# A decoder trunk on one core: norm factor as exp(-ln/2), priorities for short work, and two more pairs of projections

## The chip, the core and the metric

The kernel runs on one core of a Trainium2 chip. Its engines are TensorE (matmuls, with a sequencer that also loads the stationary operand), VectorE, ScalarE, GpSimd and SyncE; in the profile they are PE (and PEld for weight loads), DVE, ACT, POOL and SP. The metric is the device time of one execution in microseconds (us); lower is better. Before the change it is 1003.29 us, the median of three runs (1003.1 to 1003.29).

## What is computed

One layer of a decoder over 528 tokens (16 learned ones ahead of 512), 1024 channels, all in float32:

```python
u = rmsnorm(h, mix_norm_w)
proj = u @ w_in                                  # pool, z, x|B|C, dt, gates
y_pool = pool_mixer(u_pool, ...) @ w_pool_up
xbc = silu(causal_depthwise_conv(xbc, conv_w, conv_b))     # 4 taps
...                                              # 8 groups, each: 256 channels of x, 128 of B, 128 of C
y = (y_diag + y_off) + xs * d_skip               # the chunked scan
y = y * silu(z)
yg = yg * rsqrt(mean(yg * yg, per group) + EPS)  # the norm factor of this text
y_ssd = (yg * norm_w) @ w_ssd_out
h = h + (gate_pool * y_pool + gate_ssd * y_ssd) @ w_o
h = h + relu(rmsnorm(h, mlp_norm_w) @ w_ff1) ** 2 @ w_ff2
out = rmsnorm(h, final_norm_w)[16:]
```

## The kernel before

**Precision.** A float32 operand is split into a high part (ScalarE's cast, `whi`) and the rest (VectorE's subtraction, `wlo`), and a product is three matmuls: high by high, high by low, low by high. `block()` (L115) loads one 128x1024 weight block over SyncE's queue and splits it (L111, L113), with priority 100. A projection of 128 output channels (`proj`, L208) is one such block: 8 steps along the contraction, 48 matmuls of 264 columns for the 528 tokens, or 24 of 512.

**The order of the work.** The program is written in the order below, and the Tile framework then orders each engine's instructions itself: where several are ready it takes the one that was written first, and `tc.high_priority(n)` counts an instruction as written n places earlier. `tc.issue_after(i)` (and `after`, L101, for several) puts an instruction behind another one.

**The scan.** `group_tiles` (L447) gives each of the eight groups its tiles: x (`xc`, two buffers), B (`bt`), C (`ct`) and `zt`. `weave` (L729) goes by turns through the steps of `ssd(g)` (L591) and of `group_proj(g + 1)` (L530), so the projections of the next group fill TensorE while the scan of this one waits for the other engines; in group 4 the first half of the output product (`out_half`), in group 7 the rest of it (`out_part`, L839) stands beside them. `ssd` turns B and x by TensorE, makes `eb` and the decays (Exp on ScalarE, L633, L644, L645; before them Relu, L638, and VectorE's L641), the products of C and B (L656), the states (L663 to L673: ScalarE's copy `st0`, then VectorE's chain of three steps), the masked decays (L676), y (L685 to L698), the sum of squares (L703 to L710), the norm factor `rs` (L712: ScalarE's Sqrt; L714: VectorE's reciprocal in four pieces) and the normed y with its two parts `yh`, `yl` (L718 to L722).

**Pairs.** For x of groups 4 to 7 (`X_PAIRS`, L50) the two projections are done together by `pair` (L494): Strassen's seven products of half-size blocks in place of eight (`MULTIPLY`, L468), 12 matmuls of 264 columns each. Its weights are four quarters and four sums of quarters (`t1`, `s3`, `t2`, `t4`) that `weight_sums_at` (L790) has made earlier by DMAs on GpSimd's queue, some of them adding in memory; `pair_operands` (L472) loads them on SyncE's queue, two products to a block. Each product is taken out of PSUM by ScalarE or VectorE (L510 to L525) into two raw tiles, `ra` and `rb` of the pool `stg` (`raw_pair`, L527), because a bank is used again by the product after the next. `conv` (L434) then reads the raw tiles. A plain projection's `conv` reads PSUM itself. `BC_PAIRS` (L51) names the groups whose B and C would be such a pair; it is empty.

**Sums of weights.** `sets` (L761) lists what is to be summed: two sets of the pairs of the scan (`fx`), then thirteen of the MLP; `SETS_AT` (L54) says how many are made beside which group (11 in all), and L1190 makes the rest after the scan. A set of `fx` or `f1` is eight DMAs of 512 KB, one of `f2` four.

**The end of the scan.** `out_part` sums the last y products: for the first two output blocks the products with y 12 and 13 come late and alternate between both sums (L876 to L881), then `add` (L866) copies each sum out of its PSUM buffer (ScalarE, L868) and adds it to memory by GpSimd's queue (L869). The PSUM pool of these sums has two buffers.

Of the kernel before, what the change touches and what calls it, by code (L numbers as in the profile page):

```python
# [16 lines left out]
SEQ = 512  # L17
# [4 lines left out]
G = 8  # L22
# [28 lines left out]
BC_PAIRS = ()  # L51
# [13 lines left out]
def kernel(ctx: ExitStack, tc, xT, x, w, fx, f1, f2, vec, fnw, out):  # L65
# [428 lines left out]
    def pair(kind, g, r):  # L494
# [3 lines left out]
        one, two = HF  # L498
        for m, f, n, start, stop in MULTIPLY:
# [10 lines left out]
            if m == "b11":  # L510
                act.copy(r[0][:, one], o)
            elif m == "b21":
                dve.tensor_tensor(r[0][:, one], r[0][:, one], o, op=ALU.add)
            elif m == "t2":
                second_product[g] = at
                act.activation(r[1][:, one], o, AF.Copy, scale=-1.0)
            elif m == "t1":
                act.copy(r[1][:, two], o)
                yield
            elif m == "s3":  # L520
                dve.tensor_tensor(r[1][:, two], r[1][:, two], o, op=ALU.subtract)
            elif m == "b22":
                dve.tensor_tensor(r[1][:, one], r[1][:, one], o, op=ALU.add)
            else:
                act.copy(r[0][:, two], o)  # L525
# [4 lines left out]
    def group_proj(g, cur, gate=None):  # L530
# [20 lines left out]
        both = g in BC_PAIRS  # L551
        for kind, ts, paired in (("b", bcs, both), ("x", xs, g in X_PAIRS)):
            if paired:
                r = raw_pair(kind, g)
                yield from pair(kind, g, r)
                for (dst, t, skip), src in zip(ts, r):
                    conv(dst, src[:, skip:], t)
                yield
            else:
                for t in ts:  # L560
                    plain(*t)
                    filled.setdefault(g - 1, mm[0])
                    yield
            if both:
                i = 0 if kind == "b" else 1
                ps = psum2(f"pz{g}_{i}")[:, :SEQ]
                z_half(ps, i)
                z_ready[g] = act.activation(zt[:, i, :], ps, AF.Silu)
                yield
        if both:  # L570
            return
# [19 lines left out]
    def ssd(g, cur):  # L591
# [38 lines left out]
        for j in range(2):  # L630
            js = slice(64 * j, 64 * j + 64)
            with after((z_ready if g in X_PAIRS else x_ready)[g], late_cast[0] if g == G - 1 else None):
                act.activation(eb[js, :, :], ap[js, :, j, :], AF.Exp)  # L633
# [33 lines left out]
        y_first[g] = st0 = act.copy(flat(st[0]), pv[0])  # L667
# [44 lines left out]
        act.activation(rs, pn, AF.Sqrt, bias=eps, scale=1.0 / 256)  # L712
        for c in range(4):
            dve.reciprocal(rs[:, ctok(c)], rs[:, ctok(c)])  # L714
# [11 lines left out]
    late_cast, last_state = [None], {}  # L726
# [112 lines left out]
    def out_part():  # L839
# [37 lines left out]
        for o in ((0, 0), (1, 0), (0, 1)):  # L877
            for d in range(2):
                for n, (a, b) in enumerate(late[d]):
                    pe.matmul(ps[d], a[o[0]], b[o[1]], start=False, stop=o[1] == 1 and n == 1)  # L880
            yield  # L881
        for d in range(2):
            add(ps[d], d)
# [796 lines left out]
def _weight_blocks(i):  # L1680
# [15 lines left out]
    def group(g, gate_d=None):  # L1696
        z = lambda j: put(cols(w_in, OFF_Z + (2 * g + j) * P))
        both = g in BC_PAIRS
        for i, ts in enumerate(((16 + g, 24 + g), (2 * g, 2 * g + 1))):
# [3 lines left out]
            if both:  # L1703
                z(i)
        if gate_d is not None:
            gate(gate_d)
        if not both:
            for j in range(2):
                z(j)
# [122 lines left out]
```

## Time and profile before

| | |
|---|---|
| median of 3 runs | 1003.29 us |
| the profiled execution | 1003.26 us |
| its span, from the first to the last instruction | 1001.6 us |
| matmuls | 6035 |
| ScalarE's table loads | 43 |
| scan | about 75 to 475 us |
| pool branch, gates, output projection | about 475 to 675 us |
| MLP | about 675 to the end |

The profile is of one execution. A row of a timeline has the start, the duration, the engine, the source line, the operation, out<-in by the program's names, shapes and, in brackets, the idle time of the engine just before it and what ended it; xN merges N instructions. A row of the waits has the waiting engine, tile and line, what it waited for, the total, how often and the longest. A row of windows has the stretch, its length, then the busy time and count of PE, PEld, DVE, ACT and POOL, the granted clock of TensorE (1.00 throughout), the busy share of the 16 DMA engines and GB/s. The chain lists what each step was released by, back from the end. Matmuls are pipelined: a matmul's duration includes its way through the array, so two that follow each other overlap, and a TensorE that is shown busy may still be waiting a little.

### The profile page before, as it was taken

Reading aid. Unit: us, or ns where it says so; the run is one execution under the profiler, and the core shown is the slowest. Engines: PE = TensorE matmul, PEld = TensorE weight load, DVE = VectorE, ACT = ScalarE, POOL = GpSimd, SP = SyncE. Lnnn points to the kernel's source line nnn. Section 1 sums busy time; section 2 is a strip of 40 time slices with the busy share of each in tenths; the row PEclk is TensorE's granted clock in tenths of the full one; section 3 lists DMA queues with packets and bytes.
Section 4 is the critical chain, followed back from the end, with each engine's and each line's share of the span. In section 5 each row is a group of like instructions: output and inputs, shape, how many; then the busy total and the mean of one; then the engine's idle time right before and its main releaser. Section 6 shows DMA issues by size and latency. Waiting matters only on the chain.

```text
span 1001.6 us, 15673 instructions
## 1 busy us (share of the span) xinstructions
PE 989.0 (99%) x6035; PEld 873.4 (87%) x6035; DVE 804.2 (80%) x1162; ACT 602.9 (60%) x855; POOL 121.9 (12%) x215
## 2 busy tenths in 40 slices
PE   9999999999999999999999999999999999999997
PEld 7889898989889999978898888888889999999986
DVE  7977997879855888978789667876988878888885
ACT  7657749494924658574345443377666666656654
POOL 0010321211212312223200001121000000000000
PEclk9999999999999999999999999999999999999999
DMA  7374868676798849678823732889354464454332
GB/s 245 89 254 140 265 182 238 195 192 199 221 262 265 232 122 278 211 161 172 286 68 127 252 101 77 259 232 323 88 197 149 142 194 138 157 185 151 129 106 84
DMA packets 61803, 184.52 MB, mean 184 GB/s; under 512 B 7072, under 2 KB 8416, under 8 KB 60704
## 3 DMA queue, kind: packets, MB, share of 16 engines
q1 hardware_dynamic: 39456, 109.00, 33.3%
q0 software_dynamic: 18240, 67.51, 26.4%
q10 hardware_dynamic: 4032, 7.00, 1.9%
q8 instruction: 47, 0.77, 0.3%
q14 instruction: 28, 0.23, 0.1%
HBM read 173.13 MB, written 58.59 MB: 231 GB/s over the span
## 4 chain that ended last, share of the span: by engine, by line
PE 84%; DVE 7%; ACT 4%; DMA 3%; issue 1%; SPq 0%; ACTq 0%; DVEq 0%
PE px L1451 8%; PE px L215 7%; PE alpha L1519 6%; PE pz L215 6%; PE px L1454 4%; PE px L218 4%; PE pgp L215 3%; PE alpha L1522 3%; PE pz L218 3%; PE pgs L215 3%; DMA raw<-in_w 2%; PE pqx L506 2%; PE py L691 2%; PE pgp L218 2%; PE pso L146 1%; PE wo_alpha L1213 1%
## 5 line engine op out<-in xcount | busy, mean ns | idle before, releaser
L113 DVE TENSOR_TENSOR wlo<-raw,whi 128x1024 fp32r<-128x1024 f32 (+2 forms) x88 | 102.2, 1171 | 45.0 <-ACT whi L111 29.7
L111 ACT CAST whi<-raw 128x1024 fp32r<-128x1024 f32 (+2 forms) x88 | 87.2, 1012 | 64.0 <-DMA raw<-in_w 15.8
L215 PE MATMUL px<-uh,whi 128*128 128x264 f32 (+1 forms) x320 | 81.1, 291 | 0.0
L218 PE MATMUL px<-ul,whi 128*128 128x264 f32 (+1 forms) x320 | 78.7, 284 | 0.0
L1226 DVE TENSOR_TENSOR ht<-ht,alpha 128x1024 f32<-128x1024 f32 x35 | 42.7, 1220 | 29.1 <-PE alpha L1519 29.1
L215 PEld LDWEIGHTS px<-uh,whi 128*128 128x128 f32 x320 | 60.5, 189 | 1.1 <-issue 0.9
L1149 ACT CAST shi<-rawf 128x1024 fp32r<-128x1024 f32 x42 | 44.2, 1053 | 28.0 <-PE alpha L1522 18.4
L218 PEld LDWEIGHTS px<-ul,whi 128*128 128x128 f32 x320 | 60.2, 188 | 0.4 <-issue 0.2
L1519 PE MATMUL alpha<-shi,hh 128*128 128x512 f32 x140 | 55.3, 395 | 0.7 <-DVE ht L1226 0.6
L1522 PE MATMUL alpha<-shi,hl 128*128 128x512 f32 x140 | 54.7, 391 | 0.0
L1150 DVE TENSOR_TENSOR slo<-rawf,shi 128x1024 fp32r<-128x1024 f32 x42 | 51.2, 1219 | 0.6 <-ACT shi L1149 0.6
L1454 PE MATMUL px<-vsl,shi 128*128 128x256 f32 x192 | 47.4, 280 | 0.0
L1451 PE MATMUL px<-vsh,shi 128*128 128x256 f32 x192 | 47.4, 281 | 0.0
L215 PE MATMUL pz<-uh,whi 128*128 128x512 f32 x112 | 43.8, 391 | 1.7 <-DVE xc L440 1.7
L218 PE MATMUL pz<-ul,whi 128*128 128x512 f32 x112 | 43.6, 390 | 0.0
L215 PE MATMUL px<-uh,wlo 128*128 128x264 f32 (+1 forms) x320 | 42.0, 283 | 0.0
L215 PEld LDWEIGHTS px<-uh,wlo 128*128 128x128 f32 x320 | 40.0, 188 | 0.0
L1519 PE MATMUL alpha<-slo,hh 128*128 128x512 f32 x140 | 37.4, 389 | 0.0
L1451 PEld LDWEIGHTS px<-vsh,shi 128*128 128x128 f32 x192 | 36.2, 188 | 0.9
L1454 PEld LDWEIGHTS px<-vsl,shi 128*128 128x128 f32 x192 | 36.1, 188 | 0.9
L1454 PE MATMUL px<-vl,shi 128*128 128x256 f32 x144 | 36.1, 283 | 0.0
L1451 PE MATMUL px<-vh,shi 128*128 128x256 f32 x144 | 36.0, 282 | 0.0
(599 smaller groups left out, 3068.3 us busy)
## 6 DMA issues: line engine op xcount, KB each, us to landing
raw<-in_w SPq DMA_DIRECT2D x96, 512.0 KB, 4.6
f_t<-in_f POOLq DMA_DIRECT2D x38, 512.0 KB, 7.5
f_s<-in_f POOLq DMA_DIRECT2D x26, 512.0 KB, 7.0
b<-in_f SPq DMA_DIRECT2D x21, 512.0 KB, 4.4
rawf<-in_f SPq DMA_DIRECT2D x36, 256.0 KB, 3.0
rawf<-f_t SPq DMA_DIRECT2D x36, 256.0 KB, 3.1
abc<-acs_d POOLq DMA_DIRECT2D x8, 1024.0 KB, 8.3
f_t<-f_t POOLq DMA_DIRECT2D x12, 512.0 KB, 6.7
```

The source lines that it names most:

```text
L111: act.copy(hi[:, c], raw[:, c])
L113: dve.tensor_tensor(lo[:, c], raw[:, c], hi[:, c].bitcast(F32), op=ALU.subtract)
L215: pe.matmul(o, wt, rhs[0][k][:, c], start=part == 0 and k == 0, stop=part == 1 and k == NK - 1)
L218: mm[0] = pe.matmul(o, wt, rhs[1][k][:, c], start=False, stop=False)
L506: at = pe.matmul(o, wk, f[k][0], start=start and not low and k == 0, stop=stop and low == 1 and k == 3, skip_group_check=True)
L1149: splits.append((act.copy(hi, src), dve.tensor_tensor(lo, src, hi.bitcast(F32), op=ALU.subtract)))
L1150: dve.tensor_tensor(lo, src, hi.bitcast(F32), op=ALU.subtract)))
L1226: added[0] = dve.tensor_tensor(o, o, src, op=op)
L1451: pe.matmul(ps, m, f[k][0], start=start and not low and k == 0, stop=stop and low == 1 and k == 3, skip_group_check=True)
L1454: pe.matmul(ps, m, f[k][1], start=False, stop=False, skip_group_check=True)
L1519: pe.matmul(ps[t], hh[:, p, seg, st], m, start=bool(first and not low and p == 0), stop=bool(last and low and p == 1), skip_group_check=True)
L1522: pe.matmul(ps[t], hl[:, p, seg, st], m, start=False, stop=False, skip_group_check=True)
```

## The change

Five edits in the scan:

- `BC_PAIRS = (5, 6)`: B and C of groups 5 and 6 are pairs. The raw values of such a pair lie in the group's own `xc` (whose x comes later); the old form, which put z's projections between, is gone. `scan_quarters` and `sets` follow from the list: three sets of `fx` in place of two.
- The norm factor is `exp(-0.5 * ln(mean + eps))`, two ScalarE activations, in place of Sqrt and reciprocal, and `eb`'s Exp of the next group is put behind it.
- Priorities: 200 for every eviction of a pair, 60 for the states' chain, 60 for squares and their column sums, 100 for the two late sums' `add`.
- The late products of `out_part` go by output block and no longer by turns, and each block's `add` follows at once.
- `filled` (what the products of C and B wait for) is set by a pair's third product where B and C are a pair.

```diff
-BC_PAIRS = ()
+BC_PAIRS = (5, 6)
...
@@ pair @@
-            if m == "b11":
-                act.copy(r[0][:, one], o)
...
+            with tc.high_priority(200):
+                evict(m, r, o)
+            second_product.update({g: at} if m == "t2" else {})
+            if m == "t1":
                 yield
...
@@ group_proj @@
-        for kind, ts, paired in (("b", bcs, both), ("x", xs, g in X_PAIRS)):
+        for kind, ts, paired in (("b", bcs, g in BC_PAIRS), ("x", xs, g in X_PAIRS)):
             if paired:
-                r = raw_pair(kind, g)
-                yield from pair(kind, g, r)
+                r = raw_pair(kind, g) if kind == "x" else [xc[:, i, :] for i in range(2)]
+                for _ in pair(kind, g, r):
+                    filled.setdefault(g - 1, second_product[g])
+                    yield
                 for (dst, t, skip), src in zip(ts, r):
                     conv(dst, src[:, skip:], t)
                 yield
...
@@ ssd @@
-            with after((z_ready if g in X_PAIRS else x_ready)[g], late_cast[0] if g == G - 1 else None):
+            with after((z_ready if g in X_PAIRS else x_ready)[g], scaled.get(g - 1), late_cast[0] if g == G - 1 else None):
                 act.activation(eb[js, :, :], ap[js, :, j, :], AF.Exp)
...
-        y_first[g] = st0 = act.copy(flat(st[0]), pv[0])
+        with tc.high_priority(60):
+            y_first[g] = st0 = act.copy(flat(st[0]), pv[0])
...
-        for c in range(3):
-            dve.tensor_tensor(st[c + 1], st[c], bc(cdec[:, c, hs], 64), op=ALU.mult)
-            last_state[g] = dve.tensor_tensor(flat(st[c + 1]), flat(st[c + 1]), pv[c + 1], op=ALU.add)
+        with tc.high_priority(60):
+            for c in range(3):
+                dve.tensor_tensor(st[c + 1], st[c], bc(cdec[:, c, hs], 64), op=ALU.mult)
+                last_state[g] = dve.tensor_tensor(flat(st[c + 1]), flat(st[c + 1]), pv[c + 1], op=ALU.add)
...
-        squared[g] = act.activation(sq, yt, AF.Square)
-        dve.tensor_tensor(sq[:, 0, :], sq[:, 0, :], sq[:, 1, :], op=ALU.add)
-        qh, ql, halved[g] = col_sums(f"g{g}", sq[:, 0, :], gs, ("btok", "cbm"))
+        with tc.high_priority(60):
+            squared[g] = act.activation(sq, yt, AF.Square)
+            dve.tensor_tensor(sq[:, 0, :], sq[:, 0, :], sq[:, 1, :], op=ALU.add)
+            qh, ql, halved[g] = col_sums(f"g{g}", sq[:, 0, :], gs, ("btok", "cbm"))
...
-        act.activation(rs, pn, AF.Sqrt, bias=eps, scale=1.0 / 256)
-        for c in range(4):
-            dve.reciprocal(rs[:, ctok(c)], rs[:, ctok(c)])
+        act.activation(rs, pn, AF.Ln, bias=eps, scale=1.0 / 256)
+        scaled[g] = act.activation(rs, rs, AF.Exp, scale=-0.5)
...
@@ out_part @@
-        for o in ((0, 0), (1, 0), (0, 1)):
-            for d in range(2):
+        for d in range(2):
+            for o in ((0, 0), (1, 0), (0, 1)):
                 for n, (a, b) in enumerate(late[d]):
                     pe.matmul(ps[d], a[o[0]], b[o[1]], start=False, stop=o[1] == 1 and n == 1)
+            with tc.high_priority(100):
+                add(ps[d], d)
             yield
-        for d in range(2):
-            add(ps[d], d)
```

`evict` holds the seven branches that stood in `pair`, unchanged: ScalarE copies `b11`, `t2` (negated), `t1` and `t4`, VectorE adds or subtracts `b21`, `s3` and `b22`.

More of the change, by code (lines that the diff above doesn't have):

```diff
@@ L497, in pair @@
         operands = pair_operands(PAIRS.index((kind, g)))
-        one, two = HF
         for m, f, n, start, stop in MULTIPLY:
@@ L563, in group_proj @@
                     yield
[L564 to L571, printed above, removed]
         if gate is not None:
@@ L1697, in group @@
         z = lambda j: put(cols(w_in, OFF_Z + (2 * g + j) * P))
-        both = g in BC_PAIRS
         for i, ts in enumerate(((16 + g, 24 + g), (2 * g, 2 * g + 1))):
@@ L1702, in group @@
                     put(cols(w_in, OFF_XBC + t * P))
-            if both:
-                z(i)
         if gate_d is not None:
             gate(gate_d)
-        if not both:
-            for j in range(2):
-                z(j)
+        for j in range(2):
+            z(j)
     def wg(b):
```

32 lines of the change are left out of this document (17 added, 15 removed).

## The prediction, made before the result was known

> **What bounds the kernel now.** I read the page's busy times and its chain of work first, then TensorE's waits, then the timelines and windows around each wait.
>
> ```profile
> span 1001.6 us, 15673 instructions
> PE 989.0 (99%) x6035; PEld 873.4 (87%) x6035; DVE 804.2 (80%) x1162; ACT 602.9 (60%) x855; POOL 121.9 (12%) x215
> ...
> PE 84%; DVE 7%; ACT 4%; DMA 3%; issue 1%; SPq 0%; ACTq 0%; DVEq 0%
> ```
>
> TensorE is the bound: busy for 989.0 of 1001.6 us, and 84% of the chain that ends last. Its end is modelled, so the spacing of matmuls counts, not their length. What other engines cost it is in its waits:
>
> ```profile
> PE pz L215 <- DVE xc L440: 1.7, 1, 1.7
> ...
> PE psp L146 <- ACT sp L868: 1.4, 1, 1.4
> ...
> PE pz L998 <- ACT pu L1010: 0.4, 1, 0.4
> ...
> PE po L685 <- ACT st L667: 0.2, 1, 0.2
> ```
>
> (line, what it waited for, us in total, times, longest.) These four lie where the change works: 3.7 us together, each a single wait. So the diff can win in two ways alone: fewer matmuls, or these waits. Time saved on TensorE inside the scan reaches the end only if the stages behind it, TensorE-bound today, stay so.
>
> **The change part by part.**
>
> *B and C of groups 5 and 6 as pairs.* TensorE's timeline while it works on group 5's B and C and its pair for x (start, us, instruction), an eviction of such a pair, and the two groups of the page that split weight blocks:
>
> ```profile
> 317.72 2.09 PE L215 MATMUL px<-uh,wlo 128*128 128x264 f32 x16
> ...
> 326.79 0.66 PE L506 MATMUL pqx<-uh,wlop 128*128 128x264 f32 x4
> ...
> 334.08 0.65 PE L506 MATMUL pox<-t1h,wlop 128*128 128x264 f32 x4
> L511 ACT COPY rax<-pqx x4: 379/380/382, 238.0 to 408.4; 128x264 f32<-128x264 f32 x4
> ...
> L113 DVE TENSOR_TENSOR wlo<-raw,whi 128x1024 fp32r<-128x1024 f32 (+2 forms) x88 | 102.2, 1171 | 45.0 <-ACT whi L111 29.7
> L111 ACT CAST whi<-raw 128x1024 fp32r<-128x1024 f32 (+2 forms) x88 | 87.2, 1012 | 64.0 <-DMA raw<-in_w 15.8
> ...
> L215 PE MATMUL px<-uh,whi 128*128 128x264 f32 (+1 forms) x320 | 81.1, 291 | 0.0
> ```
>
> Sixteen matmuls take 2.09 us, the last of them 0.29 (the group's mean): (2.09 - 0.29) / 15 = 0.120 us apart. A plain tile has 48, so B and C take 96 x 0.120 = 11.5 us. A pair has seven products of 12; five products lie between the starts at 326.79 and 334.08, 1.46 us each, 10.2 for seven. Saved: 1.3 us a group, **2.7 us** for two (24 matmuls fewer).
>
> Added beside it, per group: 3.5 weight blocks to split in place of 2 (1.5 x 1.01 us on ScalarE, 1.5 x 1.17 on VectorE), four evictions on ScalarE (0.38 each) and three on VectorE (taken at the same): some 3 us on each engine, which the plain form lacks as its convolution reads PSUM. ScalarE hides them where it has air. It has none when group 6's pair comes, behind the start of group 5's scan:
>
> ```profile
> 348.00:358.00 10.00, 10.00 (x80) 9.79 (x78) 6.85 (x15) 9.92 (x18) 0.73 (x2) 1.00 0.43 118
> L633 ACT ACTIVATE eb<-abc 64x1024 f32<-64x1024 f32 x2 | 2.1, 1058 | 0.0
> ```
>
> (columns PE, PEld, DVE, ACT, POOL, clock, DMA). A bank is wanted again one product later, after 1.46 us. With the new priority at most the operation in progress stands ahead of an eviction: 1.06 + 0.38 = 1.44 us. That just fits; behind two operations it is late by 1.06. Bounds: nothing, and 1.06 x 8 ACT evictions = 8.5 us. The four x pairs of before run the same sequence with no wait in the list above, the nearest row: I take **+0.3 us**. That B's and C's raw values lie in the space of x costs nothing: the convolutions read them before the x convolutions, 10 us of matmuls later, write there; that cover gone, ScalarE would wait for VectorE's convolution, and with it every cast behind it. The x pairs' evictions merely move ahead, at nothing. The products of C and B (L656) now wait for the new pair's third product, 36 matmuls in, where it was 32: nothing, as other matmuls fill the place.
>
> *Norm factor.* It removes four reciprocals a group and adds one activation.
>
> ```profile
> L714 DVE RECIPROCAL rs<-rs x32: 893/895/953, 120.2 to 466.7; 128x128 f32<-128x128 f32 x32
> L712 ACT ACTIVATE rs<-png,eps x8: 687/689/692, 119.0 to 463.5; 128x512 f32<-128x512 f32 x8
> L712 ACT ACT_TABLE_LOAD x8 | 10.3, 1283 | 0.1
> 434.06 3.39 DVE L714 RECIPROCAL rs<-rs 128x128 f32<-128x128 f32 x4
> ```
>
> VectorE is relieved of 3.39 us a group; ScalarE gets an Exp, at the square root's 0.69. The square root had a table load of 1.28 us before it and the scan's Exp another; Ln and Exp keep both if they lie in two tables (that is what I take) and save one if in one. Ln and Exp were not timed here: bounds -1.28 + 0.69 = -0.6 and +0.69 + 1.28 = +2.0 us of ScalarE a group; I take +0.7. Nothing of this is on TensorE's path for groups 0 to 6: yh and yl are used only by the output products. The new order (eb's Exp behind the norm factor) puts eb of group 1 later, as it ran ahead of group 0's square root. Behind it on ScalarE stand that group's Relus, its decays' Exps and the copy of its states; the casts that TensorE's blocks need have priority 100 and pass; the py products that read its masked decays come a whole C tile later (48 x 0.120 = 5.8 us), and cover it.
>
> *The end of the scan* is where ScalarE decides (its window, TensorE's timeline, the copy's group):
>
> ```profile
> 431.00:446.50 15.50, 13.83 (x72) 10.95 (x70) 14.22 (x26) 15.39 (x25) 1.67 (x4) 1.00 0.64 181
> 440.78 1.27 PE L880 MATMUL psp<-yh,whi 128*128 128x512 f32 x4
> ...
> 442.74 0.49 PE L685 MATMUL po<-ct,st 128*128 128x128 f32 x2 [0.23 <-ACT st L667]
> ...
> 443.53 1.09 PE L880 MATMUL psp<-yl,whi 128*128 128x512 f32 x4
> 446.06 0.50 PE L146 MATMUL psp<-yh,whi 128*128 128x512 f32 x1 [1.44 <-ACT sp L868]
> ...
> L868 ACT COPY sp<-psp 128x512 f32<-128x512 f32 x2 | 1.1, 578 | 0.0
> ```
>
> ScalarE works 15.39 of 15.5 us; its copy of the first sum frees the bank for the third. The twelve late matmuls alternate between the two sums, so both finish at 444.6. Six of them are 6 x 0.23 = 1.4 us (the last four take 1.09, some 0.4 of it the tail of one). In the new order the first is done after six, 1.4 us earlier, and its copy (0.58) has priority 100, while TensorE does the other six. yh and yl come no later: Ln, load and Exp end some 2.0 us behind where the square root did, the reciprocals took 3.39. So the 1.44 goes, and most of the 0.23 (st's copy has priority 60). Against it stands the Exp, 0.69, in a full engine. Bounds: -2.0 (with the 0.3 beside them that the starts show) and +0.7. I take **-1.7 us**; what is late next is py, behind ScalarE's two Exp.
>
> *Other priorities.* The wait of 1.7 at pz is behind VectorE's convolution in group 0's stretch:
>
> ```profile
> 88.02 2.29 DVE L676 TENSOR_TENSOR abc<-abc,cbm 128x2048 f32<-128x2048 f32 x1 [2.83 <-ACT abc L644]
> 105.13 0.47 PE L215 MATMUL pz<-uh,whi 128*128 128x512 f32 x1 [1.69 <-DVE xc L440]
> ```
>
> VectorE idles 2.83 us before 88.02 and has a queue from there to the wait. The states move up in that queue, but its sum is the same: bounds -1.7 and +1.1 (an estimate, half the masking's 2.29, should a convolution stand behind the states); I take nothing.
>
> *One more set of weight sums.* Six pairs make three sets in place of two: 8 more DMAs of 512 KB on GpSimd's queue, four inside the scan and four behind it, each later set moved one place back; and 1.5 blocks more on SP's queue per group.
>
> The median load of a weight block, two stretches of the chain, windows, and the last DMA of the sums:
>
> ```profile
> raw<-in_w SPq DMA_DIRECT2D x96, 512.0 KB, 4.6
> ...
> 475.93 6.25 DMA raw<-in_w
> 482.28 1.05 ACT whi L111
> 483.33 0.29 ACT pu L1010
> 483.66 0.39 PE pz L998
> ...
> 676.02 11.68 DMA raw<-in_w
> ...
> 475.00:485.00 10.00, 9.61 (x76) 9.24 (x75) 4.82 (x6) 4.01 (x7) 3.42 (x6) 1.00 0.99 299
> 680.00:700.00 20.00, 20.00 (x90) 16.57 (x89) 10.80 (x16) 15.51 (x24) 3.53 (x5) 1.00 1.02 339
> 710.00:725.00 15.00, 15.00 (x68) 12.43 (x67) 14.70 (x25) 6.58 (x10) 0.00 (x0) 1.00 0.12 37
> ...
> 699.14 0.82 POOL L779 DMA_DIRECT2D f_s<-in_f  x1 [0.77 <-DMA f_s<-in_f]
> ```
>
> At 476 a weight load of 6.25 us holds a cast, which holds the copy that TensorE waits for; group 7's stretch now has a set of eight DMAs in place of four. On the other side that load is issued when VectorE has split the block before it, and 3.39 us of reciprocals go there. Behind the scan the sums end with the one issued at 699; four more run into 710 to 725, where the DMA engines are 12% busy. Bounds: -0.4, and +5.4 (11.68 - 6.25). I take **+0.2**.
>
> **Sum**: 1003.26 (the profiled execution, 1.66 us around its span; the median shown is 1003.29) - 2.7 + 0.3 - 1.7 + 0.2 = **999.4 us**.
>
> **The rivals.**
>
> *More than the sum* (0.18): ScalarE gets air. If Ln and Exp share one table, the full 15.5 us are 0.6 shorter and not 0.7 longer; the wait at pz (1.7) and that at L998 (0.4) go as well: 999.4 - 1.7 - 0.4 - 0.3 = 997.0. For it: DVE's idle 2.83 us before the queue. Against: st's copy stays behind the Exps that end at 88. The Trainium skill, "ScalarE: Activation LUTs", section "Table sets: the hidden batching unit", lists one set with both exp and ln, one load for the two; no Ln runs before, so no trace here shows it, and by it this rival is the likelier one.
>
> *Matmuls only* (0.20): the end of the scan gives nothing, because ScalarE stays full and its queue merely reorders what TensorE waits for, and the pairs wait a little: 1003.3 - 2.7 + 0.3 + 0.2 = 1001.1, and 1001.8 with the Exp's 0.7. For it: 15.39 of 15.5. Against: VectorE, full there as well (14.22), loses 3.39.
>
> *The pairs don't save* (0.07): evictions behind two operations in 348 to 358 return the 2.7, the order's gain stays or goes: 999.4 + 2.7 - 0.3 = 1001.8, to 1003.5. For it: 9.92 of 10 us. Against: the x pairs have no such wait.
>
> *Slower* (0.10): the added sums take the DMA engines from the weight loads. Place: the load at 476, with the share at 0.99 already; price: its 6.25 us become the 11.68 seen at 676, +5.4, and a like delay for the loads at 700; from 4 us of added delay it eats the whole gain. GpSimd's queue carries the adds of the sp sums too, so these are late with it. 999.4 + 5.4 = 1004.8, to 1008. The Trainium skill, "DMA: Bandwidth & Descriptors", section "Issuing engines are not separate DMA queues", says that DMAs of all issuers run on the same 16 engines; the rows 4.6 in the median and 11.68 at a share of 1.02 agree.
>
> **How the numbers follow.** Forecast 0.45, with 998.0 to 1000.9 as its own range. A measurement of this kernel can tell about 0.2%, 2.0 us, from no change: faster is below 1001.3. Faster: forecast 0.45, more 0.18, a third of matmuls only 0.07: 0.70. Same: the rest of it 0.13 and the pairs that don't save 0.07: 0.20. Slower 0.10. The range of 8 in 10 reaches from the larger gain with a little over (995.8) to where the sums begin to cost (1003.6).
>
> **What would show it.** Right: 6011 matmuls; rows of L506 for two pairs of B and C spaced 0.121; no wait psp <- sp; 6 reciprocals where 38 were; TensorE idle in 348 to 361 under 0.5 us. The count of table loads (43 now) tells whether Ln and Exp share one. Wrong: waits of TensorE on the evictions of the new pairs, on a cast behind a weight load near 475 or 700, or on py at the end of the scan; a gain in the scan that is gone again at 730.

## The result, and the profile after

| kernel | median, us (lowest to highest) | ratio to before (95% interval) | us by the ratio |
|---|---|---|---|
| before (4 runs) | 1003.19 (1002.27 to 1003.29) | 1 | |
| after (4 runs) | 1013.41 (1012.02 to 1015.41) | 1.0107 (1.0092 to 1.0123) | +10.7 |

The change makes the kernel slower by 1.1%; 999.4 us, with 995.8 to 1003.6, had been forecast. The ratio on record is not quite the quotient of the two medians; the differences below come from the ratios, as (ratio - 1) x 1003 us.

The page of the profiled execution of after (1012.93 us): span, busy times, chain of work.

```profile
span 1011.2 us, 15673 instructions
...
PE 991.3 (98%) x6011; PEld 874.9 (87%) x6011; DVE 782.9 (77%) x1140; ACT 616.2 (61%) x878; POOL 133.8 (13%) x227
...
PE 78%; ACT 9%; DVE 6%; issue 3%; DMA 2%; POOL 1%; ACTq 0%; DVEq 0%; SPq 0%; POOLq 0%
```

There are 6011 matmuls, as foreseen, 24 fewer than before, and yet the time is longer: TensorE's share of the chain of work fell from 84% to 78%, and ScalarE's rose from 4% to 9%. The waits of TensorE in after (waited for, us, times, longest) tell where:

```profile
PE po L685 <- DVE st L673: 2.5, 6, 0.9
PE pxx L998 <- ACT pu L1004: 2.2, 1, 2.2
PE pxx L998 <- ACT sp L868: 1.9, 1, 1.9
PE png L710 <- ACT qhg L330: 1.5, 1, 1.5
...
PE png L711 <- DVE qlg L331: 1.3, 1, 1.3
PE pqx L505 <- ACT rax L518: 1.1, 1, 1.1
```

The waits of before at pz (1.7) and psp (1.4) are gone; those above are new. To place the loss, I took the distance between the starts of successive matmuls, less the median distance that matmuls of that shape and those tiles have in before, and added up this excess in stretches of 25 us (the last two columns are runs of below):

| stretch, us | before | after | e11, order only | e18, order, loads held |
|---|---|---|---|---|
| 100 to 125 (pz on xc) | 1.99 | 0.21 | 0.14 | 0.13 |
| 125 to 150 (po on st) | -0.88 | 0.98 | -0.36 | -0.35 |
| 325 to 350 (evictions, group 5) | 0.07 | 2.50 | 0.01 | 0.02 |
| 375 to 400 (group 6) | 0.23 | 4.96 | 0.23 | 0.22 |
| 425 to 450 (end of the scan) | 2.53 | 1.95 | -0.53 | -0.69 |
| 475 to 500 (pool branch begins) | 0.68 | 6.22 | 4.92 | 0.70 |
| all of the run | 10.87 | 23.42 | 11.23 | 6.40 |

After has 12.55 us more of it; less some 2.9 us for the 24 matmuls that went (0.120 each) that is 9.7 us, and the spans differ by 9.6. Four stretches carry the loss: 125 to 150, 325 to 350, 375 to 400 and 475 to 500.

**480 to 489.** ScalarE's timeline in after (start, duration, line, what ended the idle time before it):

```profile
482.52 0.58 ACT L868 COPY sp<-psp 128x512 f32<-128x512 f32 x1 [4.87 <-DMA acc_d<-sp]
483.00 0.62 ACT L132 CAST whiB<-raw 128x512 fp32r<-128x512 f32 x1
487.63 0.58 ACT L868 COPY sp<-psp 128x512 f32<-128x512 f32 x1 [4.00 <-DMA acc_d<-sp]
488.11 0.39 ACT L1004 COPY pu<-pxx 128x264 f32<-128x264 f32 x1
```

and GpSimd's:

```profile
475.29 0.85 POOL L783 DMA_DIRECT2D f_t<-f_t  x1 [7.95 <-issue]
475.82 1.21 POOL L869 DMA_DIRECT2D acc_d<-sp  x1
...
478.54 1.61 POOL L869 DMA_DIRECT2D acc_d<-sp  x1
...
484.30 0.94 POOL L869 DMA_DIRECT2D acc_d<-sp  x1
```

The last step of the weight sums beside group 7, now a set of eight, is issued at 475.29, after GpSimd stood 7.95 us: the step ahead of it (L782, issued at 465.71) landed at 474.81. The adds of the output sums are behind it in the queue. Their staging tiles have two buffers, so ScalarE's copies wait 4.87 and 4.00 us, and `whiB` and `pu`, for which TensorE waits, stand behind the copies.

**375 to 400.** VectorE's queue and then ScalarE's in after:

```profile
363.82 1.22 DVE L113 TENSOR_TENSOR wlop<-rawp,whip 128x1024 fp32r<-128x1024 f32 x1
...
374.21 0.68 DVE L113 TENSOR_TENSOR wlop<-rawp,whip 128x512 fp32r<-128x512 f32 x1
```

```profile
381.41 1.05 ACT L111 CAST whi<-raw 128x1024 fp32r<-128x1024 f32 x1 [2.44 <-DMA raw<-in_w]
382.36 0.83 ACT L437 ACTIVATE xc<-rax,vs 128x528 f32<-128x528 f32 x1
387.52 1.05 ACT L111 CAST whip<-rawp 128x1024 fp32r<-128x1024 f32 x1 [4.33 <-DMA rawp<-in_fx]
388.48 1.05 ACT L704 ACTIVATE sqg<-yt 128x1024 f32<-128x1024 f32 x1
...
390.29 0.62 ACT L330 CAST qhg<-sqg 128x512 fp32r<-128x512 f32 x1 [0.23 <-DVE sqg L705]
```

The last subtraction of group 6's pair of B and C stands at 374.21 behind the six convolution steps of B and C, which come together only when the whole pair is done; its cast was done at 363.7. It holds a buffer of raw weights, so the next block is issued at 374.95 and lands at 381.4, and the pair for x behind it lands at 387.5. ScalarE's casts with priority 100 are ahead of the convolution and of the squares, and wait with the engine idle (2.44 and 4.33 us); `qhg` and `qlg`, and TensorE at png, wait for the squares.

**A wait costs more than itself.** Windows of after (length, busy us and count of PE, PEld, DVE, ACT, POOL, then granted clock, DMA share, GB/s):

```profile
390.00:392.00 2.00, 0.49 (x1) 0.19 (x1) 2.00 (x4) 1.71 (x4) 0.26 (x1) 1.00 0.74 277
392.00:394.00 2.00, 1.28 (x7) 1.21 (x8) 2.00 (x4) 1.98 (x3) 1.94 (x5) 0.85 0.42 91
394.00:396.00 2.00, 2.00 (x12) 2.00 (x11) 2.00 (x3) 1.97 (x3) 2.00 (x4) 0.50 0.95 329
396.00:398.00 2.00, 2.00 (x15) 1.85 (x15) 1.71 (x5) 1.99 (x3) 0.12 (x1) 0.80 1.06 255
398.00:400.00 2.00, 2.00 (x18) 2.00 (x18) 2.00 (x3) 1.60 (x4) 1.86 (x3) 1.00 1.01 240
```

TensorE is hardly busy from 389 to 392.7; then the granted clock falls to 0.50 (for 3.41 us, by the clock's own records) and is 1.00 again in the last row. The matmuls there cost 1.7 us extra, beside the 3.2 us of the two gaps. The same happens at 489, behind the waits for `whiB` and `pu`.

### The profile page after: what moved, and what is told of

Its sections match the earlier page's. It is cut to its first block, busy times and chain, and to the rows that moved or that the text cites. A ratio compares the mean times of both kernels' runs of the same rounds, so it can differ in the third digit from the quotient of the medians.

```text
span 1011.2 us, 15673 instructions
## 1 busy us (share of the span) xinstructions
PE 991.3 (98%) x6011; PEld 874.9 (87%) x6011; DVE 782.9 (77%) x1140; ACT 616.2 (61%) x878; POOL 133.8 (13%) x227
## 4 chain that ended last, share of the span: by engine, by line
PE 78%; ACT 9%; DVE 6%; issue 3%; DMA 2%; POOL 1%; ACTq 0%; DVEq 0%; SPq 0%; POOLq 0%
PE px L1451 8%; PE alpha L1519 6%; PE px L215 4%; PE px L1454 4%; PE pz L215 4%; PE alpha L1522 3%; PE pgs L215 3%; PE pgp L215 2%; PE px L218 2%; PE pz L218 2%; PE py L691 2%; PE wo_alpha L1213 1%; PE pf L146 1%; PE pso L149 1%; PE pf L147 1%
## 5 line engine op out<-in xcount | busy, mean ns | idle before, releaser
L113 DVE TENSOR_TENSOR wlo<-raw,whi 128x1024 fp32r<-128x1024 f32 (+2 forms) x84 | 97.2, 1169 | 43.7 <-ACT whi L111 39.4
L111 ACT CAST whi<-raw 128x1024 fp32r<-128x1024 f32 (+2 forms) x84 | 83.2, 1008 | 55.3 <-DMA raw<-in_w 14.4
L215 PE MATMUL px<-uh,whi 128*128 128x264 f32 (+1 forms) x256 | 66.0, 295 | 0.8 <-DVE bt L440 0.8
L218 PE MATMUL px<-ul,whi 128*128 128x264 f32 (+1 forms) x256 | 63.6, 286 | 0.0
L215 PEld LDWEIGHTS px<-uh,whi 128*128 128x128 f32 x256 | 48.9, 191 | 2.0 <-ACT whi L111 1.0
L218 PEld LDWEIGHTS px<-ul,whi 128*128 128x128 f32 x256 | 48.6, 190 | 0.1
L113 DVE TENSOR_TENSOR wlop<-rawp,whip 128x1024 fp32r<-128x1024 f32 (+1 forms) x24 | 25.9, 1087 | 21.2 <-PE pso L149 7.7
L111 ACT CAST whip<-rawp 128x1024 fp32r<-128x1024 f32 (+1 forms) x24 | 22.5, 941 | 25.4 <-PE pso L147 11.7
```

The source lines that it names most:

```text
L111: act.copy(hi[:, c], raw[:, c])
L113: dve.tensor_tensor(lo[:, c], raw[:, c], hi[:, c].bitcast(F32), op=ALU.subtract)
L215: pe.matmul(o, wt, rhs[0][k][:, c], start=part == 0 and k == 0, stop=part == 1 and k == NK - 1)
L218: mm[0] = pe.matmul(o, wt, rhs[1][k][:, c], start=False, stop=False)
```

## The experiments

**The two theories of the first four.** *Theory 1*: the new pairs cost, through what they add beside TensorE (the sums on GpSimd's queue, the loads that casts wait for). *Theory 2*: ScalarE is too full with Ln, Exp and their table loads, and the priorities order it badly. In the table, "of before" is the median of before in the same series of runs, and the last column is (ratio - 1) x 1003.

| run | kernel | median, us | of before, us | ratio (95% interval) | us |
|---|---|---|---|---|---|
| e1 | after without pairs of B and C | 1004.47 | 1002.99 | 1.0016 (1.0007 to 1.0026) | +1.6 |
| e2 | before with these pairs alone | 1011.45 | 1002.99 | 1.0086 (1.0066 to 1.0106) | +8.6 |
| e3 | after, no sums beside group 7 | 1008.99 | 1002.99 | 1.0055 (1.0039 to 1.0072) | +5.5 |
| e4 | after with square root | 1006.99 | 1002.99 | 1.0033 (1.0019 to 1.0046) | +3.3 |
| e5 | after, one set beside group 5 | 1006.79 | 1002.67 | 1.0042 (1.0027 to 1.0057) | +4.2 |
| e6 | after, eb not held | 1013.61 | 1002.67 | 1.0111 (1.0092 to 1.0130) | +11.1 |
| e7 | after: square root, fewer sums | 1003.78 | 1002.67 | 1.0015 (1.0002 to 1.0029) | +1.5 |
| e8 | before: pairs, evictions first | 1008.05 | 1002.67 | 1.0055 (1.0037 to 1.0074) | +5.5 |
| e9 | after, pairs' splits at 300 | 1010.53 | 1002.75 | 1.0080 (1.0066 to 1.0094) | +8.0 |
| e10 | before with Exp of Ln alone | 1005.00 | 1002.75 | 1.0026 (1.0015 to 1.0036) | +2.6 |
| e11 | before with the order alone | 1002.98 | 1002.75 | 1.0004 (0.9996 to 1.0013) | +0.4 |
| e12 | e4, pair in group 5 alone, no sums beside 7 | 1006.96 | 1002.75 | 1.0044 (1.0028 to 1.0060) | +4.4 |
| e13 | e11, acc loads written later | 1003.35 | 1002.79 | 1.0001 (0.9990 to 1.0013) | +0.1 |
| e14 | before, acc loads written later | 1002.80 | 1002.79 | 1.0002 (0.9991 to 1.0013) | +0.2 |
| e15 | e7, splits at 300, acc loads written later | 1003.09 | 1002.79 | 0.9991 (0.9981 to 1.0001) | -0.9 |
| e16 | e15 with Exp of Ln | 1007.31 | 1002.79 | 1.0039 (1.0025 to 1.0053) | +3.9 |
| e17 | e15, loads really held | 999.43 | 1003.18 | 0.9967 (0.9956 to 0.9978) | -3.3 |
| e18 | e13, loads really held | 997.74 | 1003.18 | 0.9949 (0.9935 to 0.9962) | -5.1 |

**e1**

```diff
-BC_PAIRS = (5, 6)
+BC_PAIRS = ()
```

> The changed kernel without the pairs for B and C (list empty again: two sets of weight sums, 6035 matmuls). Theory 1 (the pairs cost it: eight more DMAs of sums on GpSimd's queue hold the adds at the end of the scan, more weight loads hold ScalarE's casts): the waits near 328 us (2.3), 390 (3.2) and 480 to 489 (4.5) go, 10 us together, 2.7 of matmuls come back: about 1006, 1003 if nothing else is worse than before. Theory 2 (ScalarE has too much to do with Ln, Exp and their two table loads, and the priorities order it badly): these waits stay, 1013 + 2.7 or a little less, over 1010.

+1.6 in place of +10.7: as Theory 1 has it, 9.1 us come with the pairs; the waits at 390 and 480 to 489 are gone. But po on st stays (3.3 us).

**e2**, from before, with what the change does in `pair` and `group_proj` for B and C

```diff
-BC_PAIRS = ()
+BC_PAIRS = (5, 6)
```

> The kernel before with the pairs for B and C of groups 5 and 6 alone (raw values in the space of x): Sqrt and reciprocals, no new priority, late products by turns. Theory 1: it has the same waits from GpSimd's queue and the loads, 1008 to 1013. Theory 2: only the matmuls go, 1000 to 1001.

+8.6 lies in the range of Theory 1, but not by its mechanism: the largest new wait is that of TensorE for the first eviction of group 6's pair. ScalarE's timeline:

```profile
349.11 2.14 ACT L631 ACTIVATE eb<-abc 64x1024 f32<-64x1024 f32 x2
351.27 2.44 ACT L636 ACTIVATE abc<-abc,dtok 128x128 f32<-128x128 f32 x8
353.62 1.04 ACT L643 ACTIVATE abc<-abc 128x1024 f32<-128x1024 f32 x1
354.57 1.04 ACT L642 ACTIVATE abc<-abc 128x1024 f32<-128x1024 f32 x1
355.51 0.35 ACT L518 COPY xc<-pqb 128x264 f32<-128x264 f32 x1
```

Twelve scan activations and a table load stand ahead of the copy, and TensorE waits 5.5 us (with the lowered clock behind it, 7.1 us of excess in 350 to 375). A plain B has no such copy.

**e3** and **e5**, sums moved

```diff
-SETS_AT = {0: 1, 1: 1, 2: 2, 3: 1, 4: 2, 5: 2, 6: 1, 7: 1}
+SETS_AT = {0: 1, 1: 1, 2: 2, 3: 1, 4: 2, 5: 2, 6: 1, 7: 0}   # e3
+SETS_AT = {0: 1, 1: 1, 2: 2, 3: 1, 4: 2, 5: 1, 6: 1, 7: 1}   # e5
```

> The changed kernel with no set of weight sums beside group 7 (ten sets in the scan, six behind it), so that GpSimd's queue has the adds of the late sums alone there. Theory 1: the wait of TensorE for ScalarE's sp copies and what stands behind them (2.1 + 2.4 near 480 to 489) is gone: 1008 to 1009.5; what is moved behind the scan costs nothing, or shows as waits near 700 to 730. Theory 2: no more than 1 us, 1012 to 1013.5.

> After, with one set of weight sums beside group 5 in place of two (8 sum DMAs fewer there, made later). Theory A (the sums take the DMA engines from the weight loads of group 6's pair of B and C): the loads issued at 377 to 379 us, which landed at 385 to 389, land by 385, ScalarE's cast no longer holds the squares, and TensorE's waits of png on qhg and qlg (2.8 us, and the 1.7 us lost to a granted clock of 0.50 behind them) go: 1008.5 to 1010.5 us, 375 to 400 us without excess. Theory B (ScalarE's own order is at fault: the casts stand ahead of the squares whatever the loads do): 1012 to 1014 us, the png waits stay.

e3 gains 5.2 us and 475 to 500 falls from 6.22 to 0.01: the cause of the loss at 480 to 489 is shown, and nothing is lost at 700 to 730. e5 gains 6.5 us, but not as its Theory A (in the expectation above) had it: the loads issued at 377 to 379 land at 385.6 to 388.1, as in after (384.9 to 388.8), and 375 to 400 keeps 4.58. What goes is again 475 to 500 (0.01): with one set less beside group 5, the list moves and group 7 gets a set of four DMAs, as in before, not eight. Whether the sums make the loads of group 6 late isn't settled by it: two of their DMAs are still issued right ahead of these loads (375.14 and 375.82; 375.47 and 376.11 in after).

**e4**, the norm factor of before in after

```diff
-        act.activation(rs, pn, AF.Ln, bias=eps, scale=1.0 / 256)
-        scaled[g] = act.activation(rs, rs, AF.Exp, scale=-0.5)
+        act.activation(rs, pn, AF.Sqrt, bias=eps, scale=1.0 / 256)
+        for c in range(4):
+            dve.reciprocal(rs[:, ctok(c)], rs[:, ctok(c)])
```

> The changed kernel with Sqrt and the four reciprocals back and eb no longer behind the norm factor. Theory 1: 1011 to 1014. Theory 2: ScalarE has 0.7 to 2 us less a group, the waits near 328 and 390 go, 1005 to 1008.

-7.4 us against after, the number of Theory 2: po on st falls to 0.2 us, 325 to 350 to 0.07, 425 to 450 to -0.15. The stretches at 375 and 475 stay (5.16, 5.75). So both theories are true, of different stretches.

**e6** and **e10**, what of the norm factor costs

```diff
# e6, from after
-            with after((z_ready if g in X_PAIRS else x_ready)[g], scaled.get(g - 1), late_cast[0] if g == G - 1 else None):
+            with after((z_ready if g in X_PAIRS else x_ready)[g], late_cast[0] if g == G - 1 else None):
```

```diff
# e10, from before; eb's Exp behind scaled.get(g - 1) as in the change
-        act.activation(rs, pn, AF.Sqrt, bias=eps, scale=1.0 / 256)
-        for c in range(4):
-            dve.reciprocal(rs[:, ctok(c)], rs[:, ctok(c)])
+        act.activation(rs, pn, AF.Ln, bias=eps, scale=1.0 / 256)
+        scaled[g] = act.activation(rs, rs, AF.Exp, scale=-0.5)
```

> After, with eb's Exp no longer put behind the norm factor; Ln and Exp stay. If the added order is what costs (the Exps of the decays come late, VectorE's masking of 2.29 us then stands ahead of the states' chain, and TensorE waits for st): po on st falls from 2.5 to under 0.5 us, VectorE's 2.56 us of idle time ahead of the masking at 127.6 us goes, and the time is 1009 to 1011 us. If Ln, Exp and their two table loads cost by themselves: po on st stays over 2 us and the time is 1012 to 1014 us.

> Before, with the norm factor as Exp of Ln and eb's Exp behind it, nothing else. If the norm factor costs by itself (two table loads and two activations in a row, 3.9 us of ScalarE in which no eviction or cast passes): 1005 to 1008 us, with a wait of the pair's evictions near 328 us and of po on st. If it costs only beside the new pairs and priorities: 1002 to 1004 us.

e6 changes nothing (+11.1; po on st 3.1): the wait of eb isn't it, though the excess in 125 to 150 goes (-0.24) and comes back elsewhere (2.06 in 400 to 425). Ln and Exp, with `eb` behind them and nothing else, cost 2.6 us (e10). VectorE's masking of the decays, the same group in four kernels (busy, mean ns, then idle time before it), before, after, e10 and e11:

```profile
L676 DVE TENSOR_TENSOR abc<-abc,cbm 128x2048 f32<-128x2048 f32 x7 | 16.0, 2290 | 3.7 <-ACT abc L644 3.2 <-ACT abc L645 0.3
```

```profile
L676 DVE TENSOR_TENSOR abc<-abc,cbm 128x2048 f32<-128x2048 f32 x7 | 16.0, 2288 | 8.9 <-ACT abc L642 7.7 <-ACT abc L643 1.2
```

```profile
L676 DVE TENSOR_TENSOR abc<-abc,cbm 128x2048 f32<-128x2048 f32 x7 | 16.0, 2288 | 8.4 <-ACT abc L644 8.4
```

```profile
L676 DVE TENSOR_TENSOR abc<-abc,cbm 128x2048 f32<-128x2048 f32 x7 | 16.0, 2290 | 4.0 <-ACT abc L642 3.5 <-ACT abc L643 0.3
```

With Ln and Exp VectorE stands 8 to 9 us before the masking (7.5 in e6, without the wait of `eb`), without them 4: the decays' Exps come late out of ScalarE. The states' chain is behind the masking (2.29 us) in VectorE's queue, and TensorE's po waits for it. At 325 to 350 the price is another. ScalarE in after:

```profile
321.42 1.28 ACT L713 ACT_TABLE_LOAD   x1
322.71 0.69 ACT L713 ACTIVATE rs<-png,eps 128x512 f32<-128x512 f32 x1
323.42 1.28 ACT L714 ACT_TABLE_LOAD   x1
324.71 0.63 ACT L714 ACTIVATE rs<-rs 128x512 f32<-128x512 f32 x1
...
328.98 0.36 ACT L518 COPY rax<-pqx 128x264 f32<-128x264 f32 x1
```

Nothing passes in the 3.9 us of these four; the casts and copies pile up behind, and the first eviction of the pair for x is late at 328.98 (pqx on rax, 1.1 us).

**e7** and **e8**

```diff
# e7, from e4
-SETS_AT = {0: 1, 1: 1, 2: 2, 3: 1, 4: 2, 5: 2, 6: 1, 7: 1}
+SETS_AT = {0: 1, 1: 1, 2: 2, 3: 1, 4: 2, 5: 1, 6: 1, 7: 0}
# e8, from e2
-            evict(m, r, o)
+            with tc.high_priority(200):
+                evict(m, r, o)
```

> After, with the square root and reciprocals of before, one set of sums beside group 5 and none beside group 7 (both made later). If the three costs add up (6.4 us of the norm factor, 4.4 of the sums beside group 7, some 4 of those beside group 5): 997.5 to 1000.5 us, under the kernel before. If the sums that are put off only move the collision to the MLP's first loads, or another load comes late near 385: 1002 to 1005 us, with excess in 675 to 750 or still in 375 to 400.

> Before, with the pairs of B and C and the priority of 200 for evictions, nothing else. If the 5.5 us that TensorE waited for an eviction at 350 us with the pairs alone is a matter of order, it goes here together with the 1.5 us of lowered clock behind it: 1003.5 to 1006 us if nothing takes its place; if the late loads at 385 and the sums at 480 then show as in the kernel after with a square root (1007.0), 1007 to 1009 us. If priority doesn't cure it: 1010 to 1012 us.

e7 comes to +1.5, not to the 997.5 to 1000.5 us of a mere addition: 375 to 400 stays (4.30), and 475 to 500 has 2.54 although no sums are made there. e8 shows that the 5.5 us of e2 are a matter of order (no such wait), and that the late loads then come out (6.66 us in 375 to 400, 0.30 in e2).

**e9**, the late subtraction

```diff
             c = slice(0, 512 * len(ms))
-            with tc.high_priority(100):
+            with tc.high_priority(300):
                 block_split((n, raw, hi, lo), c)
```

> After, with the splits of the pairs' weight blocks at priority 300 in place of 100, so that VectorE's last subtraction of group 6's pairs (at 374.2 us, 11 us behind its cast) comes ahead of the convolutions of B and C. Theory A (that subtraction holds a raw buffer, the load behind it is issued at 374.95, and the casts that wait 2.4 and 4.3 us for the late loads hold the squares): the load is issued before 370, the casts wait under 1 us, TensorE's waits on qhg and qlg go and 375 to 400 us has under 1 us of excess: 1008 to 1010.5 us. Theory B (the loads are late because the DMA engines are full in 375 to 385, whenever they are issued): the waits stay, 1012 to 1014 us.

-2.7 us against after, between the two theories of its expectation. SyncE's queue, after and e9 (the row is of all block loads in that stretch):

```profile
363.26 12.02 SPq L95 DMA_DIRECT2D raw<-in_w  x4
```

```profile
366.12 1.53 SPq L95 DMA_DIRECT2D raw<-in_w  x2
```

The last block load of the stretch is issued by 367.7 in place of 375.3, and both waits at png are gone, as Theory A has it. But the pair for x still lands late (the casts wait 2.84 and 2.46 us), and two new waits of 1.1 us each (`ptm` on xc, `pst` on btok) stand there: 2.67 us stay of 4.96. That the full DMA engines of Theory B have a part in the rest is not shown: in 375 to 385 their share is 0.96 in after and 1.02 in e9, but 1.03 in before, which loses next to nothing there.

**e11** and **e12**. The first leaves of the change only the priorities and the new late order, the second also the pair of group 5.

```diff
# e11, from e4
-BC_PAIRS = (5, 6)
+BC_PAIRS = ()
# e12, from e4
-BC_PAIRS = (5, 6)
+BC_PAIRS = (5,)
-SETS_AT = {0: 1, 1: 1, 2: 2, 3: 1, 4: 2, 5: 2, 6: 1, 7: 1}
+SETS_AT = {0: 1, 1: 1, 2: 2, 3: 1, 4: 2, 5: 2, 6: 1, 7: 0}
```

> Before, with the priorities and the new order of the late products alone (square root, no pairs of B and C). If the prediction's account of the end of the scan is right (1.44 and 0.23 us go) and the wait at pz of 1.7 goes as it did in the kernel after: 999.5 to 1001.5 us, no wait psp on sp, none of pz on xc. If the order brings nothing without the norm factor: 1002.5 to 1004 us.

> After, with the square root, no sums beside group 7, and B and C as a pair in group 5 alone (12 matmuls fewer than before). If the waits near 389 us come from group 6's pair: 375 to 400 us without excess and 998.5 to 1001 us, below the kernel before. If group 5's pair causes them: 1003 to 1005 us with 4 us of excess there.

e12 has 0.23 in 375 to 400: the late loads belong to group 6's pair. But it and e11 lose at 475 to 500 (7.59, 4.92), where e12 makes no sums at all. e11 is the clearest: the waits at pz and psp are gone, the pool branch's first product comes 4.8 us earlier than in before (its last four matmuls start at 472.0 for 476.8), and the time is the same. ScalarE and TensorE at the loss:

```profile
480.30 1.04 ACT L111 CAST whi<-raw 128x1024 fp32r<-128x1024 f32 x1 [4.33 <-DMA raw<-in_w]
481.25 0.37 ACT L1011 COPY pu<-pz 128x264 f32<-128x264 f32 x1
...
481.67 0.59 PE L999 MATMUL pz<-t1h,whiB 128*128 128x264 f32 x1 [3.20 <-ACT pu L1011]
```

The weight load issued at 472.52 lands at 480.2: GpSimd has issued five loads of `acc` ahead of it and two more right behind, 256 KB each, and TensorE waits for the transfer. A scan that ends earlier just waits there, and the granted clock falls to 0.50 for 3.41 us.

**e13** to **e16**, the loads of acc written later: e13 is e11 with this diff, e14 before, e15 e7 with e9's diff, e16 the same as e15 but with Exp of Ln (e4's diff backwards)

```diff
-    for d in range(NK):
-        t_load = nc.gpsimd.dma_start(acc[d], acc_d[d])
...
     pend = [pooled_halves(*a) for a in pool_pair(POOL_ORDER[0])]
+    for d in range(NK):
+        with tc.issue_after(negated[POOL_ORDER[0]].ins):   # the copy of t2
+            nc.gpsimd.dma_start(acc[d], acc_d[d])
```

> The order alone (before with the priorities and the new order of the late products) with the eight loads of acc, which GpSimd issued at 468.7 to 473.3 us there, held behind the third product of the pool branch's first pair (some 476 us). If these loads take the DMA engines from the weight load that was issued at 472.5 and landed 7.7 us later, that load takes some 5 us, TensorE's wait of 3.2 us for pu and the lowered clock behind it go, and the 4.8 us by which the scan ends earlier are kept in part: 998.5 to 1000.5 us. If the load is slow for another reason, or the acc loads are then late for the sums behind: 1002 to 1004 us.

> Before, with the eight loads of acc held in the same way and nothing else. If only a scan that ends earlier runs into these loads: 1002 to 1003 us (0.4 us of wait for pu may go). If the held loads come too late for the additions behind them: 1004 to 1006 us.

> After, with the square root, the pairs' splits at 300, one set of sums beside group 5 and none beside group 7, and the loads of acc held. If the three causes found (the norm factor, the late subtraction of the pairs, the DMA engines at the end of the scan) are all there is, the 24 matmuls fewer show at last: 996.5 to 999.5 us, below the order alone with held loads. If the pairs bring a new wait wherever one is taken away: 1001 to 1004 us, and the pairs don't pay in any order tried.

> As the run before (e15), but with the norm factor as Exp of Ln. If Ln and Exp cost by themselves, this is 4 to 6.5 us above e15. If they cost only through the waits that the other edits take away: within 1.5 us of it.

The loads kept their place (468.81 us on in e13): the order behind a ScalarE instruction is an order of writing, and GpSimd, whose queue holds nothing that waits for it, runs ahead. So e13 and e14 settle nothing on contention. e15 against e16 does settle the norm factor: it costs 4.8 us beside the other edits too, although e15 itself loses 4.1 us in 475 to 500 and e16 nothing. The loss at 375 to 400 comes back: 0.27 us in e15, 4.32 in e16, where the pair for x is loaded from 376.1 us on and not from 371.8, the cast behind it waits 4.92 us, and TensorE at png waits 2.4 us for `qlg`. The same priority with Ln and Exp left 2.67 (e9), the square root without it 4.30 (e7): in the runs made, this loss goes only with both.

**e17** and **e18**, from e15 and e13: the loads of `acc`, and those of the gates behind them, stand behind a real wait of GpSimd

```diff
-        negated[p] = act.activation(r2[:, one], c, AF.Copy, scale=-1.0)
+        act.activation(r2[:, one], c, AF.Copy, scale=-1.0)
+        negated[p] = r2[:, :1]
...
+    at = pool.tensor_copy(seen, negated[POOL_ORDER[0]])   # GpSimd reads it
     for d in range(NK):
-        with tc.issue_after(negated[POOL_ORDER[0]].ins):
+        with tc.issue_after(at.ins):
             nc.gpsimd.dma_start(acc[d], acc_d[d])
...
-                with tc.issue_after(mixed[0].ins):          # the gates' loads
+                with after(mixed[0], at):
```

> As e15, but now GpSimd reads a value of the pool pair's third product before it issues the loads of acc and of the gates (in e13 to e15 these kept their place, from 469 us on, since nothing made GpSimd wait). If they take the DMA engines from the weight load issued at 473.7 (it landed at 480.6, 6.9 us): it lands in some 4.6 us, the wait of 2.4 us for pu and the lowered clock behind it (4.1 us of excess in 475 to 500) go: 997.5 to 999.5 us. If the load stays slow, or the loads put off are then late for the additions at 488: 1001 to 1004 us.

> As e13 (no pairs of B and C), with the same real wait of GpSimd. DMA contention as the cause: the load issued at 472.2 (8.9 us in e13) takes some 4.6 us, the 7.4 us of excess in 475 to 500 go for the most part: 997 to 999.5 us. Against e17 it tells what the pairs bring in the end: e17 lower by 1.5 to 2.5 us if their 24 matmuls count, equal or above if not. If the contention is not the cause: 1002 to 1004 us.

Both are faster than before. The DMA issues from 468 to 482, e11 and then e18 (count, KB each, median us to landing):

```profile
raw<-in_w SPq DMA_DIRECT2D x3, 512.0 KB, 8.9
```

```profile
raw<-in_w SPq DMA_DIRECT2D x4, 512.0 KB, 4.8
```

The same cast in e18, and GpSimd's wait there:

```profile
477.32 1.05 ACT L111 CAST whi<-raw 128x1024 fp32r<-128x1024 f32 x1 [0.73 <-DMA raw<-in_w]
```

```profile
481.16 0.65 POOL L1045 COPY seen<-pu 128x1 f32<-128x1 f32 x1 [7.53 <-DVE pu L1016]
481.75 4.29 POOL L1048 DMA_DIRECT2D acc<-acc_d  x8
```

The 4.8 us are the median of four loads; the one that the cast waits for (473.15 to 477.23) takes 4.1 us, where it took 7.7 in e11. 475 to 500 falls from 4.92 to 0.70, and the order's gain arrives: 997.74 us, 0.5% below before. Contention at the end of the scan is shown. With the pairs (e17) it is 1.8 us more, not 2.7 less; the two intervals overlap a little, but all six runs of e17 lie above all five of e18. The pairs give back 3.3 us of excess (9.73 for 6.40: some 1.0 each at 225, 350, 400 and 475) for the 2.9 of the matmuls, and don't pay in the best order tried. Whether held loads alone speed up the kernel before was not run; before has only 0.70 us of excess in 475 to 500 to lose.

## Why the prediction was wrong

- **24 matmuls fewer, -2.7**: the count was right (6011). The gain is smaller than the waits below.
- **Evictions of the new pairs, +0.3** ("a bank is wanted again one product later"): right. In 348 to 361 after's TensorE is busy all 13.00 us; without the priority it waits 5.5 us (e2), within the bound of 8.5. The x pair of group 5, whose evictions were to move "at nothing", waits 1.1 and 0.8 us for them (pqx and pox on rax); with the square root it doesn't (e4).
- **"ScalarE hides them where it has air"**, of the splits and convolutions that a pair adds: this is the step that failed first. I summed 3 us of work per engine and didn't look at the order of VectorE's queue. Convolutions that come in one lump put a subtraction 10.5 us behind its cast, that held a raw buffer, the load was late, and casts with priority held the squares: 4.7 us in 375 to 400. e12 shows that it is group 6's pair; e9 takes 2.3 of it away, and with the square root besides all of it goes (0.27 in e15).
- **The norm factor, "nothing of this is on TensorE's path for groups 0 to 6"**: failed. I followed the normed y, and py as the reader of the masked decays (they "come a whole C tile later (48 x 0.120 = 5.8 us), and cover it"). The states' chain isn't a reader of them, but it stands behind the masking in VectorE's queue, and po reads the states. Alone 2.6 us (e10), 4.8 to 7.4 beside the rest (e16 against e15, e4). The added wait of eb, to which I gave the delay, was not the cause (e6). The Trainium skill, "ScalarE: Activation LUTs", section "Table sets: the hidden batching unit", has Ln and Exp in one set with one load; here each of the eight groups has a load at L713 and one at L714, and the count is 46 where it was 43. It rises by three only, as `eb` now finds its table in five of the eight groups (3 loads at L631, 8 at L633 before). So what the rival "more than the sum" counted on did not come.
- **The end of the scan, -1.7**: right in kind with the square root, and too small: 425 to 450 goes from 2.53 to -0.53 in e11, 3.1 us and beyond the bound of -2.0. With Ln and Exp 1.95 stay. And the condition I had put at the start, that "the stages behind it, TensorE-bound today, stay so", didn't hold even then: the pool branch, right behind the scan, waits for a load (e11, e18).
- **Other priorities, nothing**: the wait at pz (1.7) went after all, in after and in e11; po on st took its place in after.
- **The added sums, +0.2**: mis-sized; 5.2 us by e3. The rival "slower" had the place, a price (5.4) and the sentence that the adds of the sp sums would be late on GpSimd's queue. That the price fits is luck: it was worked out from a weight load, and the wait is for the adds. It got 0.10 because I looked at the weight load alone; that a set of eight DMAs in place of four meets those adds was in the diff.
- **Left out altogether**: the clock. Two stretches of after, of 3.41 us each, run at 0.50, which is 1.7 us each on top of the gaps ahead of them.

## What to carry to other kernels

Before giving a change of engine time a price of nothing, list what stands behind each moved instruction in its engine's queue, whoever reads its result. Before counting time saved in a stage, look at what the next stage's first products wait for: here it was a load beside those of `acc`, and only holding these (by a real wait on the issuing engine) let 5 us arrive. And work that is put ahead must not itself wait for a transfer, as everything behind it then waits too.

## What the runs showed of the hardware

- TensorE's granted clock is halved behind gaps. In the clock records of this study's traces it falls to 0.50 in 18 stretches between 300 and 500 us: 13 last 3.41 us and five last 6.83 us, twice that. A gap is here the distance of two matmul starts beyond the usual one. All nine gaps of 2.52 to 5.66 us have such a stretch beside them (in e3 and e6 a second gap of 1.54 us follows). Below that it goes either way: 2.46 (e7) and 2.39 us (e9) have none, 1.96 and 1.61 us (e8) have one, and the same wait of 1.61 us in before has none. Two shorter gaps close together did it too (1.69 and 1.53 us in after). The Trainium skill, "TensorE: Matmul & The Clock Gate", part 1, gives half rate after at least one idle window of some 3.4 us, a window that runs freely. The length of the stretches agrees with that window. That gaps of 1.61 and 1.96 us sufficed doesn't agree with a whole window idle, and there the measurement decides; no run here shows what else the clock goes by.
- Ln and Exp each load a table (1283 ns) where they follow each other, as said above.
- With seven loads of 256 KB on GpSimd's queue beside them, three weight loads of 512 KB on SyncE's took 8.9 us in the median (e11); with these held, four took 4.8 (e18).
